# Seven block products instead of eight in the MLP up and the FFN gate and value products of a two-block transformer kernel

## The chip, the cores and the metric

The kernel runs on one core of one Trainium2 chip. The metric is the device time of one execution in microseconds. Five engines run beside each other, each in its own program order: TensorE (PE, with its weight loads shown as PEld), VectorE (DVE), ScalarE (ACT), GpSimd (POOL) and SyncE (SP), which here only issues DMA transfers. They wait for each other by semaphores.

## What is computed

512 tokens of width 1024 go through two transformer blocks in 32-bit floating point: a mixer of gated linear attention and latent attention, an MLP, a gated side input, a pooling mixer, a gated FFN with a causal convolution, a chunked attention, and a second FFN. Three stages matter here:

```python
m = rms_norm(h, mlp_norm[i])
h = h + jnp.square(jax.nn.relu(m @ w_mlp_up[i])) @ w_mlp_down[i]        # 1024 -> 4096 -> 1024
...
def conv_ffn(h, w_gate, w_val, conv_w, conv_b, w_out):                  # 1024 -> 2816 -> 1024, twice
    a = h @ w_gate
    ap = jnp.pad(a, ((0, 0), (CONV_W - 1, 0), (0, 0)))
    a = ap[:, 0:S] * conv_w[0] + ap[:, 1:S + 1] * conv_w[1] + ap[:, 2:S + 2] * conv_w[2] + conv_b
    return (jax.nn.silu(a) * (h @ w_val)) @ w_out
```

## The kernel before

Activations lie with the features on the 128 partitions and the 512 tokens along the row, so x is eight tiles of 128 x 512. Every product is made in three matmuls on two-part numbers: a float32 tile is split into a high half (ACT rounds it to the matmul's type: `wh`, `xsh`, `hh`, `yh`) and a low half (the difference, by DVE or POOL: `wl`, `xsl`, `hl`, `yl`), and `mm3` (L328) adds high x high, high x low and low x high into one PSUM bank. Of a weight block of 128 x 1024, a unit, `load_units` (L247) fetches the tile `ws` through SP, and `split_unit` (L257) makes `wh` and `wl` in two pieces of 512 columns. There are three `ws` buffers and four of `wh` and `wl`.

In the MLP and the FFNs a unit of the first product holds all eight feature tiles of the input for 128 output features; 24 matmuls of 512 columns (8 tiles x 3) fill one bank (`pup` in the MLP, `pf` in the FFN, by `product`, L1152). `finish` in `mlp` (L1184) then does relu times the norm's factor R, a square and the two halves; `gate` and `value` in `ffn` (L1348) multiply by R out of PSUM (`fa`, `fv`), do the convolution in one ACT and two DVE instructions (`fb`), silu, the product and the two halves. Of 32 MLP features tiles, groups of eight (of 22 FFN tiles, groups of eight or seven) are then multiplied with the down weights (`down`, L1142, bank `pdn`) and added into x. `weave` (L1136) puts the next group's first products ahead of a group's down products.

The order on each engine is fixed when the program is built. Generators ask for the tiles that they need, and a planner (`Pace`, L60 to L120, and `drive`, L197) keeps a running estimate of when each engine is free and each tile ready, and steps the generator of highest priority whose tiles are ready by PE's clock. `first` (L297) gives a subtraction or a product to DVE or POOL, whichever is done first by that estimate: one 512-column operation is taken as 0.60 us on DVE and 1.29 on POOL, and the two as independent. The splitter runs at most two units ahead of the matmuls after the first stage (`LAZY`).

When the stage before adds into an x tile, `after` starts `prep` (L376) on it: two halves scaled by the norm's gain, and a square that goes into the norm's sum. At the start of a stage `products` (L1162) runs two units side by side, tile by tile, as the x tiles come.

Of the kernel before, what the change touches and what calls it, by code (L numbers as in the profile page):

```python
# [16 lines left out]
P = 128  # L17
# [28 lines left out]
G1 = groups(FF1 // P, 8)  # L46
G2 = groups(FF2 // P, 8)
# [12 lines left out]
class Pace:  # L60
# [21 lines left out]
    def note(self, engine, op, args, kw):  # L82
# [29 lines left out]
        if engine == "tensor":  # L112
            self.mine.add(outs[0].tensor.name)
        self.free[engine] = start + cost
# [29 lines left out]
class Norm:  # L144


    def __init__(self, gain):
        self.gain, self.xs, self.acc, self.count = gain, [None] * KD, None, 0
        self.ms = self.r = self.R = None

# [9 lines left out]

class Block:
    NS, N3, NSM = 64, 8, 48
    NW, NL = 4, 3
# [61 lines left out]
    def slot3(self, name, dt=F32, shape=(P, 768)):  # L225
        return self.sp.tile(list(shape), dt, tag="s3", bufs=self.N3, name=name)
# [19 lines left out]

    def load_units(self, most=None):  # L247
        while self.n_load < min(self.n_split + self.NL, len(self.units)) and (most is None or self.n_load < most):
            src, cols = self.units[self.n_load]
            t = self.sp.tile([P, 1024], F32, tag="ws", bufs=self.NL, name="ws")  # L250
            if self.n_load >= self.NL:
                self.pace.ready[t.tensor.name] = self.split_at[self.n_load - self.NL]
            self.nc.sync.dma_start(t[:, :cols], src)
            self.loaded[self.n_load] = t
            self.n_load += 1

    def split_unit(self):  # L257
# [3 lines left out]
        cols = self.units[n][1]  # L261
        t = self.loaded.pop(n)
# [3 lines left out]
        if n >= self.NW:  # L266
            for x in (h, l):
                self.pace.ready[x.tensor.name] = self.freed[n - self.NW]
        for cs in (slice(0, cols // 2), slice(cols // 2, cols)):
            nc.scalar.activation(h[:, cs], t[:, cs], AF.Copy)  # L270
            self.sub(l[:, cs], t[:, cs], h[:, cs].bitcast(F32))
        self.split_at.append(self.pace.ready[l.tensor.name])
# [3 lines left out]
    def splitter(self):  # L276
        while self.n_split < len(self.units):
            yield lambda: self.n_split - self.n_free < self.NW and self.n_split - self.n_use < self.lazy
            self.load_units()
            yield [self.loaded[self.n_split]] + ([self.freed_by[self.n_split - self.NW]] if self.n_split >= self.NW else [])  # L280
            self.split_unit()

    def unit(self, *shape):
# [4 lines left out]
        cols = self.units[n][1]  # L288
# [15 lines left out]
    def sub(self, out, a, b):  # L304

        e = self.first((out, a, b), vector=(0.07, 1 / 960, 0), gpsimd=(0.1, 1 / 430, self.HELP))
        getattr(self.nc, e).tensor_sub(out, a, b)

# [67 lines left out]
    def prep(self, norm, d, x, row=True):  # L376
        yield [x]
        norm.xs[d] = self.hilo("xs", x, scale=self.col(norm.gain, d))
        self.square(norm, x, row)

# [747 lines left out]

    def units_mlp(self):
        a = self.a  # L1130
        ups = [[(a["w_up"][i], 1024) for i in g] for g in G1]
        downs = [[(a[f"w_down{gi}"][m], len(g) * 128) for m in range(KD)] for gi, g in enumerate(G1)]
        return self.weave(ups, downs)

    @staticmethod
    def weave(ups, downs):  # L1136
        out = list(ups[0])
        for i in range(1, len(ups)):
            out += ups[i] + downs[i - 1]
        return out + downs[-1]  # L1140

    def down(self, acts, after):  # L1142
        for m in range(KD):
            yield from self.unit(len(acts), 128)
            unit = self.got
            yield self.room()
            ps = self.bank("pdn")
            yield from self.fm(ps, unit, acts)
            self.used(ps)
            self.spawn(self.add_to(m, ps, after), 0)  # L1150
# [10 lines left out]

    def products(self, norm, name, finish, first):  # L1162

        if first:
            units = []
            for f in finish[:2]:
                yield from self.unit(8, 128)
                units.append(self.got)
            yield self.room()
            ps = [self.bank(name) for u in units]  # L1170
            for k in range(KD):
                yield norm.has(k)
                x = norm.xs[k]
                for i, u in enumerate(units):
                    yield [*u, *x]
                    self.mm3(ps[i], (u[0][:, k], u[1][:, k]), x, k == 0, k == KD - 1)
            for p, f in zip(ps, finish):
                self.used(p)
                self.spawn(f(p), 0)
            finish = finish[2:]  # L1180
        for f in finish:
            yield from self.product(norm, name, f)

    def mlp(self, norm, after):  # L1184
        v, s = self.nc.vector, self.nc.scalar

        def finish(acts, i, ps):
            yield norm.has_row
            yield [ps, norm.R]
            t = self.slot3("ht")[:, :T]  # L1190
            v.scalar_tensor_tensor(t, ps, 0.0, norm.R, op0=OP.max, op1=OP.mult)
            self.free()
            yield [t]
            s.activation(t, t, AF.Square)
            acts[i] = self.hilo("h", t)

        pend = None
        for gi, g in enumerate(G1):
            acts = [None] * len(g)
            yield from self.products(norm, "pup", [lambda ps, acts=acts, i=i: finish(acts, i, ps) for i in range(len(g))],  # L1200
                                     gi == 0)
            if gi == len(G1) - 1:
                norm.xs = None
                self.spawn(self.load_p(), 5)
            if pend is not None:
                yield from self.down(pend, lambda m: None)
            pend = acts
        yield from self.down(pend, after)
# [133 lines left out]
    def units_ffn(self, L):  # L1342
        a = self.a
        ups = [sum(([(a[f"w_fg{L}"][i], 1024), (a[f"w_fv{L}"][i], 1024)] for i in g), []) for g in G2]
        downs = [[(a[f"w_fo{L}_{gi}"][m], len(g) * 128) for m in range(KD)] for gi, g in enumerate(G2)]
        return self.weave(ups, downs)

    def ffn(self, L, norm, after):  # L1348
        v, s = self.nc.vector, self.nc.scalar
        cw = [lambda i, t=t: self.col(f"cw{L}", t * 22 + i) for t in range(3)]  # L1350

        def gate(i, ps, got):
            yield norm.has_row
            yield [ps, norm.R]
            a, b = self.slot3("fa")[:, :T], self.slot3("fb")[:, :T]
            v.tensor_mul(a, ps, norm.R)
            self.free()
            yield [a]
            s.activation(b, a, AF.Identity, scale=cw[2](i), bias=self.col(f"cb{L}", i))
            yield [b]  # L1360
            v.scalar_tensor_tensor(b[:, 1:], a[:, :T - 1], cw[1](i), b[:, 1:], op0=OP.mult, op1=OP.add)
            v.scalar_tensor_tensor(b[:, 2:], a[:, :T - 2], cw[0](i), b[:, 2:], op0=OP.mult, op1=OP.add)
            yield [b]
            s.activation(b, b, AF.Silu)
            got.append(b)

        def value(ps, got, acts, i):
            yield norm.has_row
            yield [ps, norm.R]
            t = self.slot("fv")  # L1370
            v.tensor_mul(t, ps, norm.R)
            self.free()
            yield lambda: got
            yield [t, *got]
            v.tensor_mul(t, t, got[0])
            acts[i] = self.hilo("y", t)

        pend = None
        for gi, g in enumerate(G2):
            acts = [None] * len(g)  # L1380
            for n, i in enumerate(g):
                got = []
                yield from self.products(norm, "pf", [lambda ps, i=i, got=got: gate(i, ps, got),
                                                      lambda ps, n=n, got=got, acts=acts: value(ps, got, acts, n)], i == 0)
            if gi == len(G2) - 1:
                norm.xs = None
            if pend is not None:
                yield from self.down(pend, lambda m: None)
            pend = acts
        yield from self.down(pend, after)  # L1390
# [121 lines left out]

    STAGES = ("mix", "mlp", "ple", "pool", "ffn0", "att", "ffn1")
    GAIN = dict(mix="attn_norm", mlp="mlp_norm", ple="ple_norm", pool="mix0", ffn0="ffn0", att="mix1", ffn1="ffn1")

    def everything(self, stages):
        nc, a = self.nc, self.a
        units = dict(mix=self.units_mix, mlp=self.units_mlp, ple=self.units_ple, pool=self.units_pool,
                     ffn0=lambda: self.units_ffn(0), att=self.units_att, ffn1=lambda: self.units_ffn(1))
        for st in stages:  # L1520
            self.units += units[st]()
        self.freed, self.freed_by, self.split_at = [], [], []
# [16 lines left out]
    def main(self, stages):  # L1539
# [4 lines left out]
        if stages[0] != "mix":  # L1544
# [3 lines left out]
            for d in range(KD):  # L1548
                self.spawn(self.prep(norm, d, self.x[d], rows.get(stages[0], True)), 0)
            if stages[0] == "ple":  # L1550
                self.spawn(self.load_p(), 0)
        for i, st in enumerate(stages):
            if i + 1 < len(stages):
# [3 lines left out]
                def after(m, nxt=nxt, row=row):  # L1557
                    self.spawn(self.prep(nxt, m, self.x[m], row), 0)
# [28 lines left out]
def pack_parts(w, parts):  # L1587
# [5 lines left out]
    return np.ascontiguousarray(np.concatenate(out))  # L1593

# [36 lines left out]
def lay_out(x, p, positions, attn_norm, w_in, gla_gate_w2, gla_gate_b, gla_out_norm, mla_q_norm, mla_w_uq, mla_kv_norm,  # L1631
# [23 lines left out]
    o["w_up"] = pack_fm(w_mlp_up[0], all8)  # L1655
    for gi, g in enumerate(G1):
        o[f"w_down{gi}"] = pack_fm(w_mlp_down[0], g)
# [4 lines left out]
    for L in range(2):  # L1662
        o[f"w_fg{L}"], o[f"w_fv{L}"] = pack_fm(ffn_w_gate_2[L], all8), pack_fm(ffn_w_val_2[L], all8)
        for gi, g in enumerate(G2):
# [44 lines left out]
```

## Time and profile before

| what | value |
|---|---|
| median of 3 runs | 1692.96 us (1687.34, 1692.96, 1693.0) |
| the profiled execution, its own time | 1687.25 us |
| its span, first to last instruction | 1685.5 us |
| mean granted TensorE clock | 0.998 |
| PE busy | 1654.5 us, 98% |
| DVE busy | 1006.8 us, 60% |
| ACT busy | 728.5 us, 43% |
| POOL busy | 192.0 us, 11% |
| HBM traffic | 90 GB/s over the span |

How to read it: matmuls are pipelined, so durations of neighbours overlap, and the pace is read from the start of one to the start of the next, or from a merged piece and its count. Idle time of an engine that isn't the one in demand costs nothing. Almost all instructions go through one recording helper and so have its line, L133; they are told apart by their tiles. The MLP runs from 265 to 618 us, the first FFN from 694 to about 1058, the second from 1316 to the end.

### The profile page before, as it was taken

The page shows a single profiled execution, that of the slowest core. Times are in us where ns is not written, and L with a number is a line of the kernel's source. Part 1 is how long each engine was busy: PE and PEld are TensorE (multiplying, and loading weights), DVE is VectorE, ACT ScalarE, POOL GpSimd, SP SyncE. Part 2 cuts the span into 40 slices and gives each one's busy share as a digit, 9 for nine tenths or more (in the row PEclk, how much of TensorE's full clock was granted, in tenths as well). Part 3 has the DMA queues.
Part 4 walks back from the last instruction along what each step waited for, and adds up shares of the span by engine and source line. Part 5 has one row for each costly group of instructions (what it writes and reads, how often), then busy time and mean ns, then how long its engine had stood idle before and what let it go on. Part 6 is the DMA issues. An engine that isn't in the chain of part 4 may idle for free. (4 is left out here: it accounts for less than half of the span.)

```text
span 1685.5 us, 22515 instructions
## 1 busy us (share of the span) xinstructions
PE 1654.5 (98%) x8696; PEld 1391.6 (83%) x8696; DVE 1006.8 (60%) x1889; ACT 728.5 (43%) x1422; POOL 192.0 (11%) x206
## 2 busy tenths in 40 slices
PE   8999999999999999999999999999999999999999
PEld 6878777888888888888888888999998788888887
DVE  6986777443434456776654645376678776644642
ACT  6746445432324245643332333375656543322321
POOL 3441302000000012200000001122221200000000
PEclk9999999999999999999999999999999999999999
DMA  6102032332333223233332332322131232333232
GB/s 214 63 26 63 16 123 75 100 101 87 102 99 113 88 88 104 75 100 98 91 111 88 96 98 94 113 76 89 64 99 53 81 101 94 100 106 95 93 98 72
DMA packets 47501, 153.73 MB, mean 91 GB/s; under 512 B 5521, under 2 KB 7458, under 8 KB 47394
## 3 DMA queue, kind: packets, MB, share of 16 engines
q1 hardware_dynamic: 47394, 152.30, 28.5%
q8 instruction: 68, 1.11, 0.3%
q14 instruction: 39, 0.32, 0.1%
HBM read 150.18 MB, written 2.10 MB: 90 GB/s over the span
## 5 line engine op out<-in xcount | busy, mean ns | idle before, releaser
L133 ACT ACTIVATE wh<-ws 128x512 fp32r<-128x512 f32 (+1 forms) x536 | 302.6, 613 | 254.7 <-PE pdn L133 214.0
L133 DVE TENSOR_TENSOR wl<-ws,wh 128x512 fp32r<-128x512 f32 (+1 forms) x508 | 341.6, 713 | 113.0 <-ACT wh L133 112.7
L133 PE MATMUL pf<-xsl,wh 128*128 128x512 f32 x704 | 275.1, 391 | 2.0 <-DVE xsl L133 2.0
L133 PE MATMUL pf<-xsh,wh 128*128 128x512 f32 x704 | 275.9, 392 | 0.0
L133 PE MATMUL pf<-xsh,wl 128*128 128x512 f32 x704 | 274.6, 390 | 0.0
L133 DVE TENSOR_TENSOR x<-x,pdn 128x512 f32<-128x512 f32 (+1 forms) x81 | 55.1, 681 | 219.1 <-PE pdn L133 219.1
L133 PEld LDWEIGHTS pf<-xsl,wh 128*128 128x128 f32 x704 | 132.6, 188 | 32.0 <-DVE xsl L133 4.3
L133 PEld LDWEIGHTS pf<-xsh,wh 128*128 128x128 f32 x704 | 132.5, 188 | 28.5 <-issue 0.5
L133 PEld LDWEIGHTS pf<-xsh,wl 128*128 128x128 f32 x704 | 132.5, 188 | 27.3
L133 PE MATMUL pdn<-yh,wh 128*128 128x512 f32 x352 | 136.9, 389 | 0.0
L133 PE MATMUL pdn<-yl,wh 128*128 128x512 f32 x352 | 136.9, 389 | 0.0
L133 PE MATMUL pdn<-yh,wl 128*128 128x512 f32 x352 | 136.9, 389 | 0.0
L133 POOL TENSOR_TENSOR sq<-sq 128x512 f32<-128x512 f32 x37 | 52.8, 1427 | 731.0 <-ACT sq L133 730.0
L133 PE MATMUL paq<-wh,xsh 128*128 128x256 f32 x384 | 111.3, 290 | 1.9 <-DVE akk L133 1.2
L133 PE MATMUL paq<-wl,xsh 128*128 128x256 f32 x384 | 108.5, 283 | 0.0
L133 PE MATMUL paq<-wh,xsl 128*128 128x256 f32 x384 | 108.5, 283 | 0.0
L133 PE MATMUL pup<-xsl,wh 128*128 128x512 f32 x256 | 99.7, 389 | 0.4 <-DVE xsl L133 0.4
L133 PE MATMUL pup<-xsh,wh 128*128 128x512 f32 x256 | 100.1, 391 | 0.0
L133 PE MATMUL pup<-xsh,wl 128*128 128x512 f32 x256 | 99.6, 389 | 0.0
L133 PE MATMUL pdn<-hh,wh 128*128 128x512 f32 x256 | 99.6, 389 | 0.0
L133 PE MATMUL pdn<-hl,wh 128*128 128x512 f32 x256 | 99.6, 389 | 0.0
L133 PE MATMUL pdn<-hh,wl 128*128 128x512 f32 x256 | 99.6, 389 | 0.0
(293 smaller groups left out, 3103.5 us busy)
## 6 DMA issues: line engine op xcount, KB each, us to landing
ws<-in_w_fg SPq DMA_DIRECT2D x44, 512.0 KB, 3.6
ws<-in_w_fv SPq DMA_DIRECT2D x44, 512.0 KB, 3.6
ws<-in_w_up SPq DMA_DIRECT2D x32, 512.0 KB, 3.5
ws<-in_w_down SPq DMA_DIRECT2D x32, 512.0 KB, 3.5
ws<-in_w_fo SPq DMA_DIRECT2D x32, 448.0 KB, 3.3
ws<-in_w_fo SPq DMA_DIRECT2D x16, 512.0 KB, 3.5
ws<-in_w_out SPq DMA_DIRECT2D x8, 512.0 KB, 3.6
ws<-in_w_gate SPq DMA_DIRECT2D x8, 512.0 KB, 3.6
```

Of the source, the lines that this page charges most:

```text
L133: return call(*args, **kw)
```

## The change

Rows and columns of the first products are blocked 2 by 2: the inputs into features 0 to 511 and 512 to 1023, the outputs (four tiles of 128: in the MLP four features tiles, in the FFN two gate and two value tiles) into two pairs, and the tokens into a left and a right half of 256. Four weight units, now packed as the four blocks of such a quad (`Quad`, `pack_quads`), give the four output tiles by seven products of 256 columns (Strassen's algorithm in Winograd's form) instead of eight. `PHASES` names the block of x that each product takes and the bank that it adds into. The weight operands are the four blocks and three sums and differences of them, which `split_unit` makes in place in `ws` and in one new tile `wx`; each is then split into halves as before. `prep_blocks` makes the seven blocks of x. `quad_step` copies partial results out of PSUM (`c1`, `u2`, `u4`) and adds them into `qx`, two tiles of 128 x 1024, from which `finish` goes on. A group that goes into the down product is now one quad (MLP: four feature tiles, FFN: two quads, four tiles; the first FFN group one quad), and its down units are woven between the next quad's products. `ws` has six buffers, slots of 128 x 512 number 55 instead of 64.

```diff
+QG1 = [1] * (FF1 // P // 4)
+QG2 = [1] + [2] * (FF2 // P // 4)
+PHASES = (("b11", 0, True), ("b21", 1, True), ("t2", 0, False), ("t3", 2, True), ("t1", 0, False), ("t4", 2, False),
+          ("b22", 0, False))
...
-    NS, N3, NSM = 64, 8, 48
-    NW, NL = 4, 3
+    NS, N3, NSM = 55, 8, 48
+    NW, NL = 4, 6
...
     def split_unit(self):
...
+        if quad and ph == 2:
+            quad.tile["s2"] = self.sp.tile([P, 1024], F32, tag="wx", bufs=1, name="wx")
         for cs in (slice(0, cols // 2), slice(cols // 2, cols)):
-            nc.scalar.activation(h[:, cs], t[:, cs], AF.Copy)
-            self.sub(l[:, cs], t[:, cs], h[:, cs].bitcast(F32))
+            if quad:
+                q = {i: t[:, cs] for i, t in quad.tile.items()}
+                if ph == 2:
+                    self.sub(q[0], q[0], q[2])
+                    self.sub(q["s2"], q[3], q[0])
+                elif ph == 4:
+                    self.add(q[2], q[2], q[3])
+                elif ph == 6:
+                    self.sub(q[1], q[1], q["s2"])
+                t = q[(0, 1, "s2", 0, 2, 3, 1)[ph]]
...
+            nc.scalar.activation(h[:, cs], t, AF.Copy)
+            self.sub(l[:, cs], t, h[:, cs].bitcast(F32))
...
+    def prep_blocks(self, norm, d, x, row=True):
...
+        self.scaled(n, x, self.col(norm.gain, d))
+        self.square(norm, x, row)
+        L, R = slice(0, T // 2), slice(T // 2, T)
...
+        if d < 4:
+            yield [n]
+            self.sub(n[:, R], n[:, R], n[:, L])
+            yield [n]
+            parts("xs", n, "b11", "t1")
+            norm.low[k] = n
+            return
+        yield [n]
+        parts("xs", n, "b21", "b22")
...
+        self.sub(c[:, L], n[:, R], low[:, R])
+        self.sub(c[:, R], c[:, L], low[:, L])
...
+        parts("xs", c, "t2", "t3")
+        self.sub(n[:, L], n[:, L], c[:, L])
...
+    def quads(self, norm, order, sizes, last, after, finish, first_of=None):
...
+            b = norm.blocks[block]
+            for k in range(4):
+                yield lambda: b[k] is not None
+                for w in range(2):
+                    yield [*unit, *b[k]]
+                    self.mm3(ps[acc][:, w * 256:(w + 1) * 256], (unit[0][:, 4 * w + k], unit[1][:, 4 * w + k]), b[k],
+                             first and k == 0 and w == 0, k == 3)
...
+    def quad_step(self, i, ps, out, kept, finish, acts, at):
...
+        if i in (0, 2, 4):
+            name = {0: "c1", 2: "u2", 4: "u4"}[i]
+            t = self.slot(name)
+            s.activation(t, ps[0], AF.Copy)
...
+            v.tensor_add(out[0][:, H[0]], ps[1], kept["c1"])
...
+            v.tensor_add(out[1][:, H[0]], ps[2], kept["u2"])
...
+            s.activation(out[0][:, H[1]], ps[0], AF.Copy)
...
+            v.tensor_add(out[1][:, H[1]], ps[2], kept["u4"])
...
     def ffn(self, L, norm, after):
...
-            v.tensor_mul(a, ps, norm.R)
...
+            self.mul(a.rearrange("p (h n) -> p h n", h=2), t4[:, :, 0, :], R3)
+            self.mul(y.rearrange("p (h n) -> p h n", h=2), t4[:, :, 1, :], R3)
```

The order of the built programs shows where it lands. First POOL, at the first FFN. Before, it has these instructions from the five squares that lead into that stage to the first of the attention behind it (`sq` sums squares, `r` and `ac` are norm factors, `bias` is a table of the attention):

```order
L133 TENSOR_TENSOR sq<-sq 128x512 x5
L133 TENSOR_TENSOR r<-ms,mhalf 128x4
L133 TENSOR_TENSOR wl<-ws,wh 128x512 x2
L133 TENSOR_TENSOR sq<-sq 128x512 x5
L133 MEMSET bias 64x64 x2
```

Now it has, in each quad from the second one on, these twelve:

```order
L139 TENSOR_TENSOR fa<-qx,R 128x512
L139 TENSOR_TENSOR ws<-ws 128x512
L139 TENSOR_TENSOR wx<-ws 128x512
L139 TENSOR_TENSOR ws<-ws 128x512 x3
L139 TENSOR_TENSOR fv<-fv,fb 128x512
L139 TENSOR_TENSOR wl<-ws,wh 128x512
L139 TENSOR_TENSOR ws<-ws,wx 128x512 x2
L139 TENSOR_TENSOR wl<-ws,wh 128x512 x2
```

Weight sums, a part of the low halves and two of a quad's gate and value operations moved to POOL; the last `wl` of the list stands just ahead of the next quad's `fa`.

Second DVE, inside the first FFN. Before, two of a group's gate and value pairs:

```order
L133 TENSOR_TENSOR wl<-ws,wh 128x512 x2
L133 TENSOR_TENSOR fa<-pf,R 128x512
L133 SCALAR_TENSOR_TENSOR fb<-fa,cols,fb 128x511
L133 SCALAR_TENSOR_TENSOR fb<-fa,cols,fb 128x510
L133 TENSOR_TENSOR wl<-ws,wh 128x512 x2
L133 TENSOR_TENSOR fv<-pf,R 128x512
L133 TENSOR_TENSOR fv<-fv,fb 128x512
L133 TENSOR_TENSOR yl<-fv,yh 128x512
```

Now, from the end of a quad's sixth product to both low halves of the next quad's third weight block:

```order
L139 TENSOR_TENSOR fa<-qx,R 128x512
L139 TENSOR_TENSOR fv<-qx,R 128x512
L139 SCALAR_TENSOR_TENSOR fb<-fa,cols,fb 128x511
L139 SCALAR_TENSOR_TENSOR fb<-fa,cols,fb 128x510
L139 TENSOR_TENSOR wl<-ws,wh 128x512
L139 TENSOR_TENSOR fv<-fv,fb 128x512
L139 TENSOR_TENSOR fv<-qx,R 128x512
L139 TENSOR_TENSOR yl<-fv,yh 128x512
L139 TENSOR_TENSOR x<-x,pdn 128x512
L139 SCALAR_TENSOR_TENSOR fb<-fa,cols,fb 128x511
L139 SCALAR_TENSOR_TENSOR fb<-fa,cols,fb 128x510
L139 TENSOR_TENSOR wl<-wx,wh 128x512
```

Ahead of the first row stands `qx`, the sum of bank and `u2`; behind the last come the second piece of `wx` and of its `wl`, so the stretch has 15 instructions. The gate and value work of a whole quad now stands between the sixth product and the `wl` of `wx`, and it reads `qx` in SBUF where it read the bank.

Third DVE, at the start of the MLP, from the x tiles' additions. Before:

```order
L133 TENSOR_TENSOR x<-x,pw 128x512 x3
L133 SCALAR_TENSOR_TENSOR xsl<-x,cols,xsh 128x512
L133 TENSOR_TENSOR x<-x,pw 128x512
L133 SCALAR_TENSOR_TENSOR xsl<-x,cols,xsh 128x512
L133 TENSOR_TENSOR wl<-ws,wh 128x512 x2
L133 SCALAR_TENSOR_TENSOR xsl<-x,cols,xsh 128x512
```

Now:

```order
L139 TENSOR_TENSOR xsl<-xn,xsh 128x512
L139 TENSOR_SCALAR xn<-x,cols 128x512
L139 TENSOR_TENSOR xsl<-xn,xsh 128x512
L139 TENSOR_TENSOR xc<-xn 128x256
L139 TENSOR_TENSOR xc<-xc,xn 128x256
L139 TENSOR_TENSOR sq<-sq 128x512 x2
L139 TENSOR_TENSOR xsl<-xn,xsh 128x512 x4
L139 TENSOR_TENSOR xc<-xn 128x256
L139 TENSOR_TENSOR xc<-xc,xn 128x256
L139 TENSOR_TENSOR xsl<-xc,xsh 128x512
```

One low half per x tile became a scaling (`xn`), for the first four tiles a difference of halves and one low half, and for the last four two low halves, three differences of half size and a low half of half size (`xc` holds t2 and t3).

## Rows read from the trace of the kernel before

**Rows 1.** The page, busy us by engine (share of span, count):

```profile
PE 1654.5 (98%) x8696; PEld 1391.6 (83%) x8696; DVE 1006.8 (60%) x1889; ACT 728.5 (43%) x1422; POOL 192.0 (11%) x206
```

**Rows 2.** The chain that ended last, in the second FFN: start us, us, what, count

```profile
1336.24 149.64 PE pf L133 x660
1485.88 43.52 PE pdn L133 x192
```

**Rows 3.** Busy us by stretch, MLP and first FFN: PE, PEld, DVE, ACT, POOL, PEclk, DMA

```profile
360.00:545.00 185.00, 185.00 (x817) 153.18 (x817) 77.73 (x122) 59.02 (x103) 0.00 (x0) 1.00 0.33 100
862.00:1058.00 196.00, 196.00 (x866) 162.28 (x866) 102.97 (x155) 64.00 (x113) 6.50 (x5) 1.00 0.31 99
```

**Rows 4.** The same chain in the attention stage, 256-column matmuls

```profile
1227.56 2.87 PE paq L133 x24
...
1242.29 3.59 PE paq L133 x30
```

**Rows 5.** Groups by form: engine, op, out<-in, shape, count | busy us, mean ns | idle

```profile
L133 PE MATMUL paq<-wh,xsh 128*128 128x256 f32 x384 | 111.3, 290 | 1.9 <-DVE akk L133 1.2 <-DVE aql L133 0.6
...
L133 PEld LDWEIGHTS paq<-wl,xsh 128*128 128x128 f32 x384 | 73.5, 191 | 0.0
...
L133 ACT ACTIVATE wh<-ws 128x512 fp32r<-128x512 f32 x470 | 268.7, 621 | 184.9 <-PE pdn L133 151.6 <-issue 20.4 <-PE pw L133 3.9
...
L133 DVE TENSOR_TENSOR wl<-ws,wh 128x512 fp32r<-128x512 f32 x442 | 300.0, 719 | 107.1 <-ACT wh L133 106.9
L133 DVE SCALAR_TENSOR_TENSOR fb<-fa,cols,fb 128x511 f32<-128x511 f32 x44 | 35.1, 798 | 33.6 <-ACT fb L133 33.6
L133 DVE SCALAR_TENSOR_TENSOR sbias<-asc,ac,bias 128x256 f32<-128x256 f32 x16 | 6.9, 476 | 0.0
L133 DVE TENSOR_SCALAR u<-u,r 128x512 f32<-128x512 f32 x8 | 3.3, 481 | 1.1 <-POOL r L133 1.1
```

**Rows 6.** Timeline of DVE, POOL idle: start us, us, instruction, count

```profile
1323.35 1.28 DVE L133 TENSOR_TENSOR wl<-ws,wh 128x512 fp32r<-128x512 f32 x2
```

**Rows 7.** Timeline of DVE and POOL, both with work, start of the MLP

```profile
266.70 5.00 POOL L133 TENSOR_TENSOR sq<-sq 128x512 f32<-128x512 f32 x3 [2.58 <-ACT sq L133]
...
268.77 3.48 DVE L133 TENSOR_TENSOR wl<-ws,wh 128x512 fp32r<-128x512 f32 x2
```

**Rows 8.** Timeline: DVE beside POOL, once on SBUF operands, once reading PSUM

```profile
668.52 1.29 POOL L133 TENSOR_TENSOR wl<-ws,wh 128x512 fp32r<-128x512 f32 x1 [3.11 <-ACT wh L133]
668.68 1.67 DVE L133 TENSOR_TENSOR x<-x,gt 128x512 f32<-128x512 f32 x1
...
659.76 1.29 POOL L133 TENSOR_TENSOR sq<-sq 128x512 f32<-128x512 f32 x1 [1.97 <-ACT sq L133]
659.81 0.68 DVE L133 TENSOR_TENSOR gt<-pgt,R 128x512 f32<-128x512 f32 x1
```

**Rows 9.** Timeline at the MLP's start, DVE and PE; in brackets the wait

```profile
258.45 1.28 DVE L133 TENSOR_TENSOR x<-x,pw 128x512 f32<-128x512 f32 x2
...
265.35 0.39 PE L133 MATMUL pup<-xsh,wh 128*128 128x512 f32 x1
...
272.97 0.50 PE L133 MATMUL pup<-xsl,wh 128*128 128x512 f32 x1 [0.43 <-DVE xsl L133]
...
276.10 1.05 PE L133 MATMUL pst<-ones,sq 128*128 128x1 f32 x8 [1.70 <-DVE sq L133]
```

**Rows 10.** PE at the second FFN's start: timeline, then the stretch with its PEclk

```profile
1325.95 0.50 PE L133 MATMUL pf<-xsl,wh 128*128 128x512 f32 x1 [0.81 <-DVE xsl L133]
...
1327.82 1.05 PE L133 MATMUL pst<-ones,sq 128*128 128x1 f32 x8 [1.14 <-DVE sq L133]
...
1330.74 0.63 PE L133 MATMUL pf<-xsl,wh 128*128 128x512 f32 x1
1331.16 0.63 PE L133 MATMUL pf<-xsh,wl 128*128 128x512 f32 x1
...
1330.10:1333.50 3.40, 3.40 (x10) 2.62 (x9) 2.08 (x6) 1.15 (x2) 0.07 (x1) 0.50 0.08 25
```

More of the change, by code (lines that the diff above doesn't have):

```diff
@@ L113, in note @@
             self.mine.add(outs[0].tensor.name)
+            start = max(start, self.open.get(outs[0].tensor.name, (0, 0.0))[1])
         self.free[engine] = start + cost
@@ L149, in __init__ @@
         self.ms = self.r = self.R = None
+        self.low, self.blocks = [None] * 4, {b: [None] * 4 for b, _, _ in PHASES}
     def has(self, k):
@@ L307, in sub, with add @@
         getattr(self.nc, e).tensor_sub(out, a, b)
+    def add(self, out, a, b):
+        e = self.first((out, a, b), vector=(0.07, 1 / 960, 0), gpsimd=(0.1, 1 / 430, self.HELP))
+        getattr(self.nc, e).tensor_add(out, a, b)
     def mul(self, out, a, b):
@@ L1126, in mix, with units_quads @@
         self.att = self.og = self.gg = self.vg = self.gq = self.gk = self.la = self.qpad = None
+    @staticmethod
+    def units_quads(src, downs, sizes):
+        quads, units, order, wait = [Quad(src[4 * i:4 * i + 4]) for i in range(sum(sizes))], [], [], []
+        q = 0
+        for g, n in enumerate(sizes):
+            rest = len(wait)
+            for i in range(n):
+                last = g == len(sizes) - 1 and i == n - 1
+                for ph in range(7):
+                    order.append((q, ph))
+                    units.append(("quad", quads[q], ph))
+                    put = (ph == 4) + (ph == 6 and not last)
+                    if n == 1 and not last:
+                        put += ph in (2, 3)
+                    for _ in range(min(put, len(wait))):
+                        order.append(wait[0][:2])
+                        units.append(wait.pop(0)[2])
+                q += 1
+            for w in wait:
+                order.append(w[:2])
+                units.append(w[2])
+            wait = [("down", (g, u), x) for u, x in enumerate(downs[g])]
+        for w in wait:
+            order.append(w[:2])
+            units.append(w[2])
+        return units, order
@@ new lines, in down, with halves_of @@
+    def down(self, acts, u, after):
+        n = len(acts)
+        yield from self.unit(8, P)
+        unit = self.got
+        for i in range(8 // n):
+            yield self.room()
+            ps = self.bank("pdn")
+            yield from self.fm(ps, unit, acts, i * n, n)
+            if i == 8 // n - 1:
+                self.used(ps)
+            self.spawn(self.add_to(8 // n * u + i, ps, after), 0)
+    @staticmethod
+    def halves_of(t):
+        return t.rearrange("p (h w n) -> p h w n", h=2, w=2)
@@ L1129, in units_mlp @@
     def units_mlp(self):
         a = self.a
[L1131 to L1150, printed above, removed]
+        at, downs = 0, []
@@ L1160, in product @@
         self.spawn(finish(ps), 0)
[L1162 to L1208, printed above, removed]
     def units_ple(self):
@@ L1363, in gate @@
+            v.scalar_tensor_tensor(b[:, 2:], a[:, :T - 2], cw[0](f), b[:, 2:], op0=OP.mult, op1=OP.add)
             yield [b]
             s.activation(b, b, AF.Silu)
[L1365 to L1389, printed above, removed]
@@ L1390, in ffn @@
-        yield from self.down(pend, after)
+            yield [b, y]
+            self.mul(y, y, b)
+            yield [y]
+            acts[i] = self.hilo("y", y)
+        first = {}
+        yield from self.quads(norm, self.order["ffn", L], QG2, 2, after, finish, first)
+        norm.blocks = None
     def units_att(self):
@@ L1548, in main @@
             for d in range(KD):
[L1549 removed]
+                prep = self.prep_blocks if stages[0] in self.QUADS else self.prep
+                self.spawn(prep(norm, d, self.x[d], rows.get(stages[0], True)), 0)
             if stages[0] == "ple":
```

213 lines of the change are left out of this document (182 added, 31 removed).

## The prediction, made before the changed kernel had run

> **What bounds the kernel now.** I read the page first: TensorE (PE) is busy 98% of the span, VectorE (DVE) 60%, ScalarE (ACT) 43%, GpSimd (POOL) 11% [rows 1]. A busy PE need not be a PE at its pace, so I read the end of the chain of waits next: in the second FFN it is only PE, 660 gate and value matmuls in 149.64 us, then 192 of the down product in 43.52 us [rows 2]. That is 226.7 ns from one 512-column matmul to the next in both (149.64 / 660, 43.52 / 192), with no wait between them. The stretches inside the MLP and inside the first FFN say the same: PE busy 185.00 of 185.00 us and 196.00 of 196.00 us, while POOL has nothing at all in the one and five short additions in the other [rows 3]. So in the three stages that the change touches, matmuls set the time, and an element-wise instruction costs nothing as long as it is ready before its matmul.
>
> **What PE saves.** A quad (four weight tiles) was 4 x 24 = 96 matmuls of 512 columns: 96 x 0.2267 = 21.76 us. It becomes seven products of 24 matmuls of 256 columns. The price of a 256-column matmul is read where the kernel already has them in a row, in the attention projections: 30 in 3.59 us and 24 in 2.87 us [rows 4], 119.7 ns each, a little over half of 226.7. The duration of 290 ns in the groups is longer than that pitch because matmuls overlap, and must not be used as a price; nor is the weight load (191 ns) a floor, since these matmuls load new weights each, as those of the changed kernel will [rows 5]. So a quad costs 168 x 0.1197 = 20.11 us. There are 8 quads in the MLP and 11 in each FFN, 30 in all: 30 x (21.76 - 20.11) = **49.5 us** saved. Seven eighths of the arithmetic would be 81.6 us; the rest goes into the shorter matmuls' poorer pitch. The down products keep their matmuls.
>
> The Trainium skill (TensorE: Matmul & The Clock Gate, section "Wait — 56ns, not 53.3ns?") gives the pitch as N / 2.4 GHz plus a fixed 2.5 ns. By that figure a quad would fall from 20.71 to 18.35 us, and the saving would be an estimated 71 us; the trace shows some 13 ns over N / 2.4 GHz at both sizes [rows 2, 4], so the sum goes by the rows.
>
> **What it adds, and what hides it.** Per quad of an FFN the order of the changed program has 33 instructions on DVE and 12 on POOL: 14 low halves of the seven weight blocks, 8 sums and differences of weight tiles, 12 for the gate and value (they now read SBUF, not PSUM), 4 low halves for down, 3 block sums and 4 additions into x that read PSUM. ACT gets some 170 more conversions of weights and 120 copies out of PSUM in the whole kernel, at 621 ns [rows 5]: 180 us on an engine that stands idle for over 950, hidden but for its place in one chain below. The twice as many additions into x (a partial sum every two or four feature tiles, not eight) are in the 33. The loads are the same bytes through the same queue, at about 30% of the DMA engines [rows 3], and I cost them at nothing; they are hidden behind six buffers.
>
> On DVE an unhindered 512-column operation in a row of them takes 0.64 us (two in 1.28) [rows 6], so 33 are 21 us against 31.0 us of PE per FFN quad (20.11 plus 48 x 0.2267 = 10.88 for its share of down). That looks hidden. It is not, because of **what DVE and POOL do to each other**. Where DVE subtracts SBUF tiles while POOL adds others, DVE takes 3.48 us for two where it takes 1.28 alone, and POOL 5.00 for three [rows 7]: they take turns, a pair in about 1.71 us. x<-x,gt took 1.67 us beside a POOL operation of 1.29 us that had begun 0.16 us earlier, and ended only after it. One that reads PSUM is not held: gt<-pgt took 0.68 us in the middle of a POOL addition [rows 8]. So each POOL operation with a DVE operation of two SBUF operands behind it costs DVE 1.71 - 0.64 = 1.07 us. The planner's costs (`first`, `note`) know nothing of this; they give work to POOL as if it were free.
>
> The Trainium skill (SBUF — State Buffer, "Who interferes with whom") has this as a rule: a DVE instruction with two SBUF inputs and a GpSimd instruction that reads SBUF share one read interface under an exclusive lock. The trace agrees (1.67 against 0.68 us), and it is the rule that speaks against this change.
>
> **FFN, quads 2 to 11 of each.** The dangerous chain runs from the end of product 6 to the weights of product 3 (tile wx, the difference of differences). In between DVE has 15 instructions in order (the second piece of order in the section on the change), POOL seven (wl, fa, ws, wx, ws three times). Free, DVE needs 15 x 0.64 = 9.6, 0.4 for four slower fb operations, and 0.7 for ACT's conversion between the two halves of wx: 10.7 us. PE meanwhile does product 7, a down unit and products 1 and 2: 3 x 2.87 + 5.44 = 14.05 us. Free, it is hidden with 3.3 us to spare. Blocked, seven POOL operations add 7 x 1.07 = 7.5: 18.2 us, and PE waits **4.1 us per quad**. It does not get ahead later, since the chain starts again from PE's own product 6. 20 such quads: **82 us**. The bounds are 0 (all fits between) and, with the clock, 114 (below). I take 82, since rows 7 show strict turns whenever both queues are full, and here both are.
>
> **MLP, quads 2 to 8.** PE has 41.9 us per quad (20.11 + 96 x 0.2267), the plan puts the wx differences a product earlier, and relu needs no POOL. DVE has about 37 instructions per quad and POOL 9: 37 x 0.64 + 9 x 1.07 = 33 us. I take 0, up to 8 us over the stage.
>
> **The three starts.** The first quad needs the blocks of x: scaled, differenced and split in two more combinations. In the MLP DVE has 42 instructions from the first finished x to the last low half of combination t2, which product 3 needs: 29 x 0.64, 4 scalings at 0.48 and 9 half-size ones at about 0.41 (estimates from u<-u,r and the 256-column sbias [rows 5]) make 24.2 us; 17 POOL additions can add 8 x 1.07 + 9 x 0.55 = 13.5. From 258.45, where that x is added [rows 9], it ends between 282.7 and 296. PE finishes the stage before at 265.35 and has three products, 8.6 us, until 274.0. So it waits 9 to 22 us, where it now waits 0.43 + 1.70 = 2.1 [rows 9]. I take 14 more per start, as the eight additions of x read PSUM and give POOL room: 3 x 14 = **42 us** (20 to 60).
>
> **Sum.** -49.5 + 82 + 42 = +74.5 on the profiled 1687.25 is 1762; the median of the runs stands 5.7 above that profiled run, which gives 1767. I put **1765 us**, between the two: slower.
>
> **Rivals.** (a) *The blocks find gaps.* If POOL's operations mostly fall where DVE waits for ACT or reads PSUM, PE waits at most 0.5 us per quad and 6 per start: -49.5 + 10 + 18 = -21, some 1670. For it: DVE alone has 10 us of room per quad. Against: fifteen DVE instructions stand beside seven of POOL without a wait on PE but one. The point is 0.4 us of waiting per FFN quad with starts at 14, 1.6 with starts at 6; between these two it is no change. (b) *The clock falls too.* After PE idled 0.81 and 1.14 us at the start of the second FFN the granted clock stood at 0.50, its lower level of 1.2 GHz, for 3.4 us, and matmuls came every 0.43 us [rows 10]: about 1.6 us lost. Waits of 4 us are longer; one such fall per FFN quad adds 32: 1797. For it: the wait was half as long there. Against: idles of 0.43 and 1.70 us at 272 [rows 9] brought no fall. The Trainium skill (TensorE: Matmul & The Clock Gate, "Why this matters for your kernels") warns of idle gaps between bursts of matmuls; whether waits as regular as these do it, no row here shows. (c) *A 256-column matmul as long as its weight load*, 191 ns: a quad would be 32 us, 330 us lost. The rows exclude it, since loads and matmuls overlap there. (d) *It doesn't do what it says*: excluded, as the order has 168 matmuls of 256 columns per quad and no pf or pup.
>
> **How the numbers follow.** Forecast 0.49 (1735 to 1790), slower still by the clock 0.27 (1785 to 1820), small loss 0.04 (1702 to 1735), no change 0.07, faster 0.13 (1655 to 1684). Measurement tells about 0.5% from no change, 8 us. Slower 0.80, same 0.07, faster 0.13. Range 1690 to 1820: it leaves out the faster case and a little above.
>
> **What would show it.** After: PE in FFN waits on wl<-wx once per quad, near 4 us; DVE wl and fb means go from 0.72 and 0.80 to over 1 us (now [rows 5]); the pq matmuls keep 120 ns where they run without waits; POOL is busy over 600 us; long waits at the first quad of each stage on xsl. Wrong would be: PE in FFN with no waits on wx (the chain's free length holds, rival a), DVE durations unchanged beside a busy POOL (no turns), or waits mainly on ws transfers, which I cost at nothing.

## The result: 11.7% slower, and the profile after

| | before | changed |
|---|---|---|
| median of 4 runs, us | 1692.98 | 1888.88 (1887.85 to 1889.12) |
| span of the profiled execution | 1685.5 | 1886.9 |
| ratio to before, 95% interval | 1 | 1.1165 [1.1141, 1.1188] |
| mean granted TensorE clock | 0.998 | 0.944 |

The direction was forecast, the size was not: 196 us more where I put 72, and above the range. The page of the changed kernel, to be held against [rows 1], with the granted clock in 40 slices (tenths):

```profile
PE 1690.5 (90%) x10856; PEld 1521.1 (81%) x10856; DVE 1400.7 (74%) x2181; ACT 896.5 (48%) x1745; POOL 738.6 (39%) x585
PEclk9999998999999997899999899999997899999899
```

DVE has 394 us more, POOL 547 us more. The three stages show where the time went. Both kernels, one row per stage (MLP, first FFN with the last product of the stage ahead, second FFN): stretch, its length, busy us of PE, PEld, DVE, ACT and POOL with counts, PEclk, DMA share, GB/s. First before:

```profile
265.35:618.17 352.82, 350.69 (x1548) 289.57 (x1547) 164.42 (x249) 126.24 (x219) 12.38 (x9) 1.00 0.31 97
687.25:1058.72 371.47, 370.24 (x1662) 306.01 (x1661) 218.27 (x328) 142.92 (x246) 18.66 (x14) 1.00 0.30 96
1316.50:1681.72 365.22, 363.27 (x1595) 299.28 (x1593) 197.01 (x300) 122.08 (x210) 8.49 (x6) 1.00 0.29 93
```

and after:

```profile
272.23:641.45 369.22, 350.29 (x2122) 315.01 (x2122) 246.98 (x342) 171.91 (x307) 138.86 (x103) 0.97 0.29 96
716.95:1176.68 459.73, 389.57 (x2454) 359.17 (x2453) 370.34 (x425) 201.25 (x360) 223.21 (x147) 0.90 0.24 80
1437.10:1883.23 446.13, 377.89 (x2387) 348.89 (x2385) 351.94 (x395) 182.16 (x326) 216.45 (x142) 0.90 0.23 75
```

The MLP lost 16.4 us, the FFNs 88.3 and 80.9. Length less PE busy is PE's waiting: 5.3 us before, 157.3 after. Laid over the clock's records, 154.6 us of PE's busy time after stand at a granted clock of 0.50 (before: 3.4). There a 256-column matmul takes 0.21 us (the stretch below) in place of 0.12, and a 512-column one 0.43 in place of 0.23 [rows 2, 4, 10]. So 0.44 or 0.47 of that time is lost, by the counts of both about 69 us (before: 1.6). What is left of PE's busy time is 1082.6 before and 1048.8 after. So the account of the spans is:

| term | forecast, us | measured, us |
|---|---|---|
| PE's work | -49.5 | -34 |
| waits inside the three stages | +124 | +152 |
| lower clock | 0 (rival b: 32) | +67 |
| stages that begin later after the one ahead | in the 124 | +16 |
| sum | +74.5 | +201 |

(The 16: the MLP's first product comes at 272.23 in place of 265.35, the gaps between the stages are 6.4 and 2.6 longer.) What PE waits for, changed kernel: waiting tile and releaser, us in total, times, longest:

```profile
PE pq L139 <- ACT c L139: 72.2, 26, 4.4
PE pdn L139 <- ACT yh L139: 27.4, 6, 5.3
PE pq L139 <- ACT xsh L139: 19.3, 4, 10.3
...
PE pq L139 <- DVE xsl L139: 10.9, 6, 4.4
PE pst L139 <- DVE sq L139: 10.2, 4, 5.2
```

The first row is mostly the wait at product 3, once in each FFN quad from the second on: 68.1 us of it in 20 quads, 14 of them with 3.8 us each; the other 4.1 us are in the MLP. One of them, from the timeline (start us, us, engine, instruction, in brackets the wait ahead of it); the rows are picked from the 18 us behind product 6, which ended at 1063.8:

```profile
1068.00 1.74 POOL L139 TENSOR_TENSOR fa<-qx,R 128x512 f32<-128x512 f32 x1
1068.50 1.78 DVE L139 TENSOR_TENSOR wl<-ws,wh 128x512 fp32r<-128x512 f32 x1
1069.69 1.74 POOL L139 TENSOR_TENSOR ws<-ws 128x512 f32<-128x512 f32 x1
1070.21 1.77 DVE L139 TENSOR_TENSOR fv<-fv,fb 128x512 f32<-128x512 f32 x1
1071.51 1.63 POOL L139 TENSOR_TENSOR wx<-ws 128x512 f32<-128x512 f32 x1
1071.90 1.78 DVE L139 TENSOR_TENSOR fv<-qx,R 128x512 f32<-128x512 f32 x1
1073.10 5.13 POOL L139 TENSOR_TENSOR ws<-ws 128x512 f32<-128x512 f32 x3
...
1075.32 0.68 DVE L139 TENSOR_TENSOR x<-x,pdn 128x512 f32<-128x512 f32 x1
...
1079.31 0.68 DVE L139 TENSOR_TENSOR wx<-ws 128x512 f32<-128x512 f32 x1
1080.02 0.63 ACT L139 ACTIVATE wh<-wx 128x512 fp32r<-128x512 f32 x1 [6.15 <-DVE wx L139]
1080.55 0.61 ACT L139 ACTIVATE fb<-fb 128x512 f32<-128x512 f32 x1
1080.68 0.69 DVE L139 TENSOR_TENSOR wl<-wx,wh 128x512 fp32r<-128x512 f32 x1 [0.70 <-ACT wh L139]
1081.07 0.58 ACT L139 ACTIVATE c<-pq 128x512 f32<-128x512 f32 x1
1081.70 0.58 PE L139 MATMUL pq<-xsh,wh 128*128 128x256 f32 x1 [3.81 <-ACT c L139]
```

Beside a busy POOL, DVE's instructions on SBUF tiles come one every 1.7 us and last 1.77 or 1.78, POOL's 1.63 to 1.74; the one that reads a bank (`x<-x,pdn`) takes 0.68 in between. These are the turns of [rows 7, 8], met four and more in a row. The last low half of `wx` ends at 1081.37, 17.5 us behind product 6 (forecast 18.2), and PE has waited 3.81 us (forecast 4.1). The releaser that the row names is another: `c`, the copy of product 1's bank, on which product 3 adds. It stands on ACT behind the conversion of `wx` and ends at 1081.65, 0.3 us after the weights. Two chains end there at almost the same time, of which I had costed one.

In this wait the clock falls, 2.5 us after PE's last matmul ended. The stretch with the lower clock, columns as in the stages' rows:

```profile
1080.39:1087.21 6.82, 5.51 (x26) 5.51 (x27) 6.30 (x9) 4.90 (x10) 4.17 (x3) 0.50 0.33 99
```

For 6.82 us PE is granted 0.50, the level of 1.2 GHz, and is busy for 5.51 of them: 26 matmuls take 0.21 us each in place of 0.12, so 2.4 us are lost. The fall is twice as long as the 3.4 us of [rows 10] in ten of the 14 quads that wait 3.8 us; in four it lasts 3.4 us, and 1.5 are lost. From product 3 to product 3 a quad then takes 37.5 us (31.3 of work, 3.8 of waiting, 2.4 by the clock), or with the shorter fall 36.6:

```profile
932.42:969.06 36.64, 32.82 (x216) 30.70 (x217) 30.52 (x34) 15.69 (x29) 19.16 (x13) 0.94 0.27 87
```

### The profile page after: what moved, and what is told of

Same layout as the page of the kernel before. It is cut to its first block, busy times and chain, and to the rows that moved or that the text cites. A ratio compares the mean times of both kernels' runs of the same rounds, so it can differ in the third digit from the quotient of the medians.

```text
span 1886.9 us, 28181 instructions
## 1 busy us (share of the span) xinstructions
PE 1690.5 (90%) x10856; PEld 1521.1 (81%) x10856; DVE 1400.7 (74%) x2181; ACT 896.5 (48%) x1745; POOL 738.6 (39%) x585
## 4 chain that ended last, share of the span: by engine, by line
PE 54%; DVE 28%; ACT 8%; issue 7%; POOL 2%; DMA 0%; SPq 0%; DVEq 0%; ACTq 0%; POOLq 0%
PE pq L139 18%; PE pdn L139 14%; DVE wl L139 6%; PE paq L139 6%; DVE qx L139 3%; DVE fv L139 3%; PE pw L139 3%; DVE fb L139 2%; DVE x L139 2%; PE pgv L139 2%; DVE yl L139 2%; ACT wh L139 2%; PE pgt L139 2%; ACT fb L139 2%; PE pl L139 1%
## 5 line engine op out<-in xcount | busy, mean ns | idle before, releaser
L139 PE MATMUL pq<-xsh,wh 128*128 128x256 f32 x1440 | 438.0, 304 | 96.1 <-ACT c L139 72.2
L139 ACT ACTIVATE wh<-ws 128x512 fp32r<-128x512 f32 x648 | 367.8, 621 | 258.8 <-PE pdn L139 107.2
L139 DVE TENSOR_TENSOR wl<-ws,wh 128x512 fp32r<-128x512 f32 x529 | 415.7, 823 | 77.7 <-ACT wh L139 75.1
L139 PE MATMUL pq<-xsl,wh 128*128 128x256 f32 x1440 | 431.0, 299 | 11.0 <-DVE xsl L139 10.9
L139 PE MATMUL pq<-xsh,wl 128*128 128x256 f32 x1440 | 429.5, 298 | 0.0
L139 POOL TENSOR_TENSOR wl<-ws,wh 128x512 fp32r<-128x512 f32 x119 | 164.6, 1388 | 614.6 <-ACT wh L139 451.6
L139 PEld LDWEIGHTS pq<-xsh,wh 128*128 128x128 f32 x1440 | 300.9, 209 | 106.0 <-ACT c L139 77.5
L139 PEld LDWEIGHTS pq<-xsl,wh 128*128 128x128 f32 x1440 | 300.8, 209 | 15.4 <-DVE xsl L139 12.7
L139 PEld LDWEIGHTS pq<-xsh,wl 128*128 128x128 f32 x1440 | 299.7, 208 | 0.0
L139 POOL TENSOR_TENSOR ws<-ws 128x512 f32<-128x512 f32 x102 | 173.1, 1711 | 42.3 <-DVE wl L139 42.3
L139 PE MATMUL pdn<-yh,wh 128*128 128x512 f32 x352 | 143.7, 408 | 27.4 <-ACT yh L139 27.4
```

Of the source, the lines that this page charges most:

```text
L139: return call(*args, **kw)
```

## The experiments

Ratios are to the kernel before, with 95% intervals; times are medians of four runs. My theory was that the sums' element-wise work, through the turns, is late and the late weights stall PE; its rivals were that PE is held by something else of the new scheme (copies out of the banks, the order on ACT), and that the clock falls for another reason than the waits.

**e1: nothing of the quads on POOL.**

```diff
-            self.sub(l[:, cs], t, h[:, cs].bitcast(F32))
+            nc.vector.tensor_sub(l[:, cs], t, h[:, cs].bitcast(F32))
...
-            self.mul(y, y, b)
+            v.tensor_mul(y, y, b)
```

> The weight sums and differences, all low halves, the block differences, gate and value go to DVE; POOL keeps only the squares and what the attention stages gave it before. If DVE and POOL take turns: from the end of product 6 to the second low half of wx DVE has 20 instructions, 20 x 0.64 + 0.4 + about 1.4 for two conversions = 14.6 us against 14.05 of PE, so PE waits some 0.6 us per FFN quad instead of 3.8, the clock has less to fall for, the starts lose some of their wait: about 1760 us. If DVE's instructions are as slow as in the changed kernel for another reason (15 took some 18 us), 20 of them take 24 us, the wait grows to 10 us per quad: over 2000 us.

Measured 1883.04 us, 1.1143 [1.112, 1.1167]: neither theory's time. The same two whole-kernel rows of DVE, by form (busy us, mean ns | idle), of the changed kernel and then, in the second fence, of e1:

```profile
L139 DVE TENSOR_TENSOR wl<-ws,wh 128x512 fp32r<-128x512 f32 x527 | 413.5, 822 | 77.7 <-ACT wh L139 75.1
...
L139 DVE SCALAR_TENSOR_TENSOR fb<-fa,cols,fb 128x510 f32<-128x510 f32 x44 | 71.2, 1619 | 1.6
```

```profile
L139 DVE TENSOR_TENSOR wl<-ws,wh 128x512 fp32r<-128x512 f32 x646 | 428.6, 700 | 159.0 <-ACT wh L139 158.5
...
L139 DVE SCALAR_TENSOR_TENSOR fb<-fa,cols,fb 128x510 f32<-128x510 f32 x44 | 33.0, 750 | 1.6
```

A steady quad of e1 as a stretch, columns as in the stages' rows, and its wait at product 3:

```profile
1014.90:1049.80 34.90, 31.81 (x216) 29.18 (x216) 28.56 (x45) 15.93 (x29) 0.00 (x0) 1.00 0.28 91
...
1016.10 0.39 PE L139 MATMUL pq<-xsh,wh 128*128 128x256 f32 x1 [1.21 <-ACT c L139]
```

The turns are gone (822 to 700 ns, 1619 to 750 ns), product 3 waits 1.21 us in place of 3.81, the clock stays at 1.00, and the quad is 34.9 us, not 37.5. But DVE now has 45 instructions per quad, and two other places of the quad wait 0.6 and 1.3 to 1.4 us (below, with e8). The MLP's steady quads, which had waited 0.18 us, now wait 1.28 each, and the second to fourth quad of each FFN wait up to 8.9; I put that down to DVE being still behind from the start. So the turns make most of the wait at product 3, and removing them by giving the work to DVE gains nothing on the whole.

**e2: idle matmuls in the place of the wait.**

```diff
+            if i == 1 and what and first_of is not None:
+                ps[2] = self.bank("pq2")
+                for j in range(32):
+                    self.nc.tensor.real.matmul(ps[2][:, :256], unit[0][:, j % 8], b[j % 4][0], start=True, stop=True,
+                                               skip_group_check=True)
             self.used(ps[acc])
```

> From the second quad of each FFN on, 32 matmuls that nobody reads stand between products 2 and 3 (into a bank that product 4 clears anyway); 32 x 0.1197 = 3.83 us, as long as the wait there. If the wait is what lowers the clock: no fall in those quads, each about 2.7 us shorter, 20 x 2.7 = 54: about 1835 us. If the clock falls for another reason (short matmuls, the quad's mean pace): falls as before, 1889 us or a little more.

Measured 1857.34 us, 1.0995 [1.0977, 1.1013]: 31.5 us faster with 640 matmuls more. Three and a bit quads of it as one stretch:

```profile
980.00:1095.00 115.00, 115.00 (x810) 107.98 (x810) 98.06 (x109) 50.56 (x90) 59.41 (x38) 1.00 0.28 90
```

No wait and no fall. So the wait is what lowers the clock. The time is 22 us over what I had written because two or three quads of each FFN wait elsewhere (on `yh`, up to 5.4 us) and the added matmuls only cost there: in both FFNs 76.8 us were added (20 x 3.84), and 69.4 us of waits and 39 us by the clock went, 32 us net.

**e3: three units ahead**, and **e4: e1 and e3 together.**

```diff
-    LAZY = 3, 2
+    LAZY = 3, 3
```

> The splitter may run three units ahead of the matmuls, not two; the planner then puts the weights of product 3 ahead of the gate and value work. If the order alone makes the wait: it goes, and the clock stays up, 20 x (3.8 + 2.7) = 130 less: about 1760 us. If DVE and POOL take turns: a quad's 34 instructions on DVE and 11 on POOL are 34 x 0.64 + 11 x 1.07 = 33.5 us against 31.0 of PE, so 2.5 us of wait per quad go to other products and some clock falls stay: about 1840 us.

> Both edits together: nothing of the quads on POOL, three units ahead. If turns are the cause: 45 instructions x 0.64 + 0.8 = 29.6 us on DVE per FFN quad fit into 31.0 of PE and no chain is late: the FFN quads run at PE's pace with the clock up, about 1740 us, the rest being the starts. If DVE is simply overloaded: over 1830 us.

Measured 1959.5 us, 1.1595 [1.1578, 1.1612], and 1991.98 us, 1.179 [1.1772, 1.1807]. e4 is where its second theory put it, over 1830. e3 is slower than either of its theories allowed, and 71 us slower than the changed kernel. The timeline of e3 at its wait:

```profile
1041.85 1.55 DVE L139 TENSOR_TENSOR wl<-wx,wh 128x512 fp32r<-128x512 f32 x1 [0.15 <-ACT wh L139]
...
1050.41 0.63 ACT L139 ACTIVATE fb<-fb 128x512 f32<-128x512 f32 x1 [1.50 <-DVE fb L139]
...
1051.12 1.52 POOL L139 TENSOR_TENSOR fv<-fv,fb 128x512 f32<-128x512 f32 x1 [1.35 <-ACT fb L139]
...
1052.61 1.71 POOL L139 TENSOR_TENSOR ws<-ws 128x512 f32<-128x512 f32 x1
...
1054.35 0.63 ACT L139 ACTIVATE wh<-ws 128x512 fp32r<-128x512 f32 x1 [0.44 <-POOL ws L139]
1054.88 0.58 ACT L139 ACTIVATE c<-pq 128x512 f32<-128x512 f32 x1
...
1055.52 0.58 PE L139 MATMUL pq<-xsh,wh 128*128 128x256 f32 x1 [5.08 <-ACT c L139]
```

The weights of product 3 are early now (the first row is the last low half of `wx`, done at 1043.40), but `c` stands on ACT behind conversions of the weights of products 4 and 5. The last of these waits for a sum on POOL (product 5's), and that stands on POOL behind `fv`, which waits for silu on ACT. The copy that PE needs next was put in line behind work for later.

**e9: e3 with the copies first**, and **e10: e4 with the copies first.**

```diff
+            u = self.units[self.n_split]
+            if isinstance(u[0], str) and u[2] in (3, 5):
+                yield lambda: (u[1], {3: "c1", 5: "u2"}[u[2]]) in self.done
```

> As e3, but the splitter doesn't put the weights of products 4 and 6 in line before the copies c and u2 out of PSUM are in line on ACT. In e3 PE waited 5.1 us per FFN quad for the copy c, which stood in ACT's queue behind two conversions of weights that were not ready. If that order on ACT is what made e3 slower: c comes 4 us sooner, the wait falls to about 1 us per quad and the clock stays up, also in the MLP (3.2 us per quad in e3): 1959 - 20 x (4 + 2.5) - 6 x 3 - 6 = about 1800. If DVE and POOL together have too much to do: the wait moves to the next product that lacks its weights, over 1880.

> The same on top of e4 (all on DVE, three units ahead), which waited 4.1 us per FFN quad and 4.75 per MLP quad, on c and on the low halves of y and h. If the order on ACT is the cause there too: 1992 - 20 x (3.5 + 2) - 6 x 4 = about 1860, and 1800 if the waits on yh go with it. If DVE's own queue is: over 1930.

Measured 1846.09 us, 1.0928 [1.0901, 1.0955]: 113 us less than e3 and 43 less than the changed kernel; nothing is left out in it. That lies between the two cases that I had written. Two steady quads, and one's wait at product 3:

```profile
1004.40:1070.80 66.40, 63.64 (x432) 58.63 (x432) 60.99 (x67) 32.43 (x57) 39.57 (x25) 1.00 0.28 96
...
1038.56 0.39 PE L139 MATMUL pq<-xsh,wh 128*128 128x256 f32 x1 [0.94 <-ACT c L139]
```

33.2 us per quad, one wait of 0.94 and several under 0.3, no fall. That is close to what I had worked out for e3 as DVE's and POOL's own time under turns, 33.5 us, and DVE is busy for 30.5 of the 33.2. So the quad may now go at DVE's and POOL's pace, over PE's 31.0; no run shows that alone. e10 measured 1966.88, 1.1645 [1.1619, 1.1672], where the second theory put it (DVE's own queue): PE waits 77 us for `yh` and 66 for `qx`.

**e5: without the weights' sums.**

```diff
-                if ph == 2:
-                    self.sub(q[0], q[0], q[2])
...
-                t = q[(0, 1, "s2", 0, 2, 3, 1)[ph]]
+                t = q[(0, 1, 3, 0, 2, 3, 1)[ph]]
```

> Leaves out the eight sums and differences of weight tiles in each quad (wx is not made; products 3, 4, 5 and 7 take a plain block), so the output is not the network's. PE does the same matmuls. If the wait per quad comes from the element-wise work that the sums add, beside POOL: POOL has four or five operations in the stretch behind product 6 in place of seven, 10.7 + 4 x 1.07 = 15 us against 14.05, the wait falls from 3.8 to 1 us or less and the clock stays up: about 1889 - 20 x (2.8 + 2.7) = 1780. If PE is held by the copies out of its own banks (c, u, qx), which are all still there: over 1850.

Measured 1717.41 us, 1.0155 [1.014, 1.0171]. A stretch inside its first FFN:

```profile
800.00:1040.00 240.00, 240.00 (x1678) 225.57 (x1678) 187.49 (x243) 124.10 (x222) 71.44 (x47) 1.00 0.31 105
```

1678 matmuls without a wait, 30.9 us per quad of 216, as forecast for PE alone (31.0). In that stretch the copies `c` and `u`, `qx` in SBUF and the POOL instructions that stay do no harm. Leaving out the eight sums per quad gives back 171 of the 196 us lost, 108 in waits and 54 by the clock by the same account as above. The time is 63 us under the 1780 that I had written, which counted only the wait at product 3 and the falls with it.

**e6: without the blocks of x**, and **e7: without either.**

```diff
-            self.sub(n[:, R], n[:, R], n[:, L])
...
+            norm.blocks["t2"][k] = norm.blocks["t4"][k] = norm.blocks["b21"][k]
+            norm.blocks["t3"][k] = norm.blocks["b22"][k]
```

> Leaves out the sums and differences of x at the three starts (the products take halves of x as they are), so the output is not the network's; the weights' sums stay. By my sum the starts cost 14 us each from 42 instructions on DVE and 17 on POOL, of which 16 differences and 12 low halves go: the starts lose some 12 us each with what the clock adds, 1889 - 36 to 45 = about 1847. If the starts wait for other things (the squares and the norm, the first weights, the first group's down product), it falls by less than 15: over 1874.

> Leaves out both, the weights' and x's sums. PE's work is that of the changed kernel. If these sums make all of the loss, what stays is the seven products' saving: 1693 - 49 = 1644, or up to 1690 with some waits left at the starts. If reading qx from SBUF and the copies out of PSUM cost as much by themselves: over 1730.

Measured 1866.13 us, 1.1035 [1.1019, 1.1052], and 1702.84 us, 1.0067 [1.0052, 1.0082]. e6 lies between what I had written for the two cases: the differences cost 23 us. e7 shows what this order of the scheme would give with free sums: it is still 13 us (0.7%) slower than the kernel before, between the two cases that I had written. Its stages:

```profile
271.43:620.92 349.49, 343.07 (x2123) 310.25 (x2121) 205.29 (x319) 166.02 (x296) 51.99 (x40) 0.99 0.30 101
695.68:1070.11 374.43, 359.18 (x2454) 335.18 (x2453) 291.78 (x384) 198.17 (x353) 110.98 (x75) 0.98 0.29 98
1330.47:1694.13 363.66, 350.71 (x2387) 326.03 (x2385) 272.93 (x359) 176.93 (x316) 100.64 (x68) 0.98 0.28 93
```

PE is busy 1053.0 us, 30.0 of them at the lower clock, so about 1040 at full clock against 1082.6: some 43 us are saved in truth. They go into 34.6 us of waits (5.3 before), 12 us more by the clock and 14 us of later beginnings. One of the waits, which comes in every variant at the end of an FFN (1.3 us in e8, 5.3 in e3 and e9):

```profile
1670.81 0.79 PE L139 MATMUL pdn<-yh,wh 128*128 128x512 f32 x1 [4.49 <-ACT yh L139]
```

Between the last quad's last product and this matmul PE has only 30 matmuls of the down product, 6.8 us, while that quad's first halves come 11.3 us after its last product.

**e8: e1 without the multiplication by R** (gate and value are taken from `qx` as they are, which is laid out so that they can be read in place).

```diff
-            self.mul(a.rearrange("p (h n) -> p h n", h=2), t4[:, :, 0, :], R3)
-            self.mul(y.rearrange("p (h n) -> p h n", h=2), t4[:, :, 1, :], R3)
+            a, y0 = t[:, :T], t[:, T:]
```

> All quad work on DVE as in e1, and the FFN's gate and value are not multiplied by the norm's factor R (left out, so the output is not the network's; qx is laid out so that they can be read in place). From the end of product 6 to the second low half of wx there are 16 DVE instructions in place of 20: 16 x 0.64 + 0.4 + 1.4 = 12.0 us, under PE's 14.05. If that chain makes the waits of e1 (3.1 us per quad): they go, FFN quads take 31.0 us in place of 35.0, about 1883 - 70 = 1810. If the waits come from the queue of DVE and ACT as a whole: some 1 us per quad goes, 1850 to 1865.

Measured 1856.79 us, 1.0979 [1.096, 1.0997]: the second theory. PE's waits in e1 and in e8:

```profile
PE pq L139 <- ACT c L139: 40.3, 27, 3.0
PE pq L139 <- DVE qx L139: 38.7, 19, 4.9
...
PE pq L139 <- ACT u L139: 15.4, 21, 2.6
```

```profile
PE pq L139 <- DVE qx L139: 39.3, 19, 4.9
...
PE pq L139 <- ACT c L139: 20.0, 27, 2.8
PE pq L139 <- ACT u L139: 17.6, 22, 1.7
```

Four instructions fewer ahead of `wx` take the wait at product 3 away in the steady FFN quads (0.18 us is left of 1.21); those for `u` and `qx`, later in the quad, don't move.

## Why the size was wrong

- **PE's saving** (49.5 us): the pitch of 119.7 ns held (30.9 us per FFN quad in e5, forecast 31.0), and e7 saves 43 us. In the changed kernel only 34 are saved; a steady quad there has 31.3 us of work. No run separates where the missing us go.
- **The wait per FFN quad** (4.1 us, 82 in all): right in mechanism and nearly in size. It is 3.81 us where the quads are steady and 68 us over the 20 quads, by the turns of DVE and POOL (822 to 700 ns without POOL, and 1.21 us of wait) on the chain that I had named. What it missed is `c`, which ends 0.3 us after the weights: PE needs both, and in e3, where the weights are early, `c` is late for a reason of its own.
- **The clock**: the step that failed. I set the clock beside the forecast as a rival with 0.27, priced at 1.6 us per fall from [rows 10]. It is a consequence of the waits that I forecast (e2), in every FFN quad from the second on, at 2.4 us each in most of the steady ones, and at the starts too: 67 us in all that the sum had at nothing. With them it would have been +142 us, of the +201 measured. The row that I held against it, idles of 0.43 and 1.70 us without a fall [rows 9], was of waits less than half as long. Waits of 0.9 to 1.4 us per quad (e1, e9) brought no fall in the steady quads, those of 3.8 us did each time. In between it is mixed: 2.1 us in each of the MLP's steady quads in e9 brought none, 3.2 us in e3's MLP brought one in every second quad, and a wait of 2.14 us in the second FFN quad of the changed kernel brought one.
- **The starts** (42 us): mis-sized. Inside the stages PE waits 13.5, 18.6 and 16.7 us in its first quad, 49 together against some 5 before, and the stages begin 16 us later: about 59. Leaving out the differences of x gives back 23 us, with what the clock adds (e6). Of the rest, the longest waits that e6 keeps at the starts are for the high halves of x, 9.3 and 5.4 us in the two FFNs.
- **Left out**: the down product's wait for `yh`, 27.4 us in six places: 5.3 in the second quad of each FFN, 3.9 in the fourth, 4.5 at the end. At the end only 6.8 us of matmuls lie between. In the other two places five products lie between a group's last product and its first down unit, and its halves are late all the same.
- **The rivals**: the blocks don't find gaps (a); with nothing but PE's work, the weights' low halves and the gate and value they would (e5). (c) and (d) are excluded as argued.

The turns and the wait at product 3 were the forecast's. Its own terms at their measured prices (-34 for PE's work, 72 for all the waits on `c`, 59 for the starts) make about 98 of the 201 us, and the two terms that its sum did not have (67 for the clock, 27 for `yh`) about 95; the other 9 us are waits of 0.2 to 1.8 us for `u`, `qx`, `hh` and low halves.

Does any variant beat the kernel before? The best complete one is e9 at 1846. e7, with both kinds of sums for nothing, is still at 1703 in the changed kernel's order, so I don't expect another order of this work to win unless it also shortens the waits at the starts and the ends of the stages. That is not shown: I did not try to run the first quad of a stage in the old way, nor a planner that counts the turns of DVE and POOL.

## What to carry to other kernels

A scheme that trades matmuls for additions has to be priced on the engines that add: here 1.65 us of PE per quad were bought with eight more sums of weight tiles, besides the copies and additions of the results, on engines that had looked half idle. Where one forecasts a wait of several us between matmuls in every round, the lower clock that came with it here belongs into the sum, not beside it. And a copy that PE's next product waits for should be in line ahead of work for later products: moving it alone was worth 113 us here (e3 to e9).

## What I had not expected of the hardware

With a wait of 3.8 us came a fall of the granted clock of 6.8 us (in four of 14 quads, 3.4), so that the quad was 6.6 us (5.7) longer than the 30.9 us of e5, not 3.8. Matmuls that nobody reads, in the place of the wait, keep the clock at 1.00 and made the kernel 31.5 us faster (e2). And `fb<-fa,cols,fb`, which reads two SBUF tiles, seems to take turns with POOL as the plain subtractions do: the one of 510 columns takes 1619 ns on the mean in the changed kernel and 750 in e1, with nothing of the quads on POOL.
